# Sums of squares folded on VectorE, a third buffer for a tile of scales, and one integer step fewer in a streaming hybrid layer

## The chip, the cores and the metric

The kernel runs on one core of a Trainium2 chip. Its time is the device time of one execution in microseconds (us). The kernel before takes 2223.6 us, the median of three runs (2219.76, 2223.6 and 2225.92 us). The profiler took one more execution, which lasted 2219.34 us, and all lines of the profile come from that one.

TensorE (PE) multiplies matrices into PSUM. VectorE (DVE), ScalarE (ACT) and GpSimd (POOL) do the elementwise work. The queue of SyncE (SP) issues nearly all transfers.

## The reference, cut to what matters

One layer on 2112 tokens of width 1024 (2048 prompt frames and 64 frames of a running stream): a norm, one input projection, a gated delta rule and a pooling group, an output projection, a residual add, a second norm, a gated feed-forward part, a residual add and a final norm. The change touches how operands are brought into range for 16-bit products, above all in the feed-forward part, whose hidden width is 22 tiles of 128:

```python
h = rmsnorm(x, norm2_w)
x = x + (silu(h @ w_gate) * (h @ w_up)) @ w_down
```

## The kernel before, in words

**Precision.** A product in nearly full precision is made of three products of 16-bit parts. Every operand x is split into a high part hi = f16(c·x) and a low part lo = f16(c·x − hi) (`split16`, lines 907 to 910: the high part on ScalarE, the low part on VectorE), and hi·hi, hi·lo and lo·hi are summed in PSUM. The scale c is a power of two that depends on the size of the operand, and it is found on the chip.

**Finding a scale.** `scale_of` (lines 621 to 627) starts from a tile `squares` of 128 partitions and n columns, each column being a sum of squares that ScalarE wrote with its accumulator. It copies the n columns to bf16 on VectorE (`cols`, with the names `sqb` or `sqe` in the profile), then issues n products on TensorE, one per column, each against the same 128x128 matrix of one value; they add up in one column of PSUM, so that all partitions hold the total. `half_power` (lines 614 to 619) then makes a power of two of the total with integer steps on the bits: add 1e-30 (PSUM to SBUF), shift right by one and mask to the exponent, subtract from a constant. The square root of the total is so halved in its exponent and inverted.

`scale_of` is called for:
- the 22 tiles of gate and up weights, n = 4 (`prep_strassen`, line 809; PSUM tile `ws`, result `pscale`);
- the 22 tiles of down weights, n = 2 (`down_scale`, line 903; `wd`, `dscale`);
- the 8 tiles of output-projection weights, n = 2 (`convert`, line 850; `wcwout`);
- the 15 groups of hidden activations, n = 2G, that is 8 or 4 (`factors`, line 1986; `ec`, result in the tile `es`);
- three single sums, n = 1 (lines 634 and 881).

`half_power` is also called for the 21 scales of the input projection together and for one scale of the output projection (lines 870 and 890).

**Feed-forward stage.** It runs from about 940 us to the end. The tokens are cut into three blocks b = 0, 1, 2 of 704, each of two halves of 352 columns. In each block the 22 hidden tiles are made one after the other (`gate_up`: seven Strassen products of 12 matmuls each, tiles `px`, `py`, `pz`), and they form six groups of sizes 4, 4, 4, 4, 2, 4. When the last tile of a group is made, `factors` (lines 1981 to 2005) finds the group's scale into `es`, a tile of six columns, and splits seven combinations of the hidden tiles per pair into the f16 tiles `hq` and `h7` (seven operations on ScalarE and seven on VectorE for a pair; four subtractions on GpSimd before them). Later `down_strassen` (lines 2007 to 2027) multiplies the parts with the down weights (tiles `dx`, `dy`, `dz`) and adds the results into the residual tiles `y` with VectorE, and each of these additions reads a column of `es`. The down products of groups 0, 1 and 2 come one hidden tile after their group is complete; those of groups 3, 4 and 5 all come at the end of the block. Block 0 treats groups 0 and 4 without this scale, and block 2 group 5.

**Buffers.** `es` has two buffers, `h7` four, the f32 scratch tag `t` eight (`tmp` in `factors`, and the loads of the next block's hidden inputs, `xh`, share it). A third `es` tile can be written only when the first is released by its last reader.

**Order.** Nothing is issued as it is written. The class `Machine` records every operation, models engines and buffers, and writes out its own order for each engine (line 374, which is why all instructions have that line in the profile). It goes through the list in windows of 1000 operations and plays each window 40 times with randomly moved ranks from one generator with a fixed seed, and keeps the ranks that lose the least TensorE time (`issue`, lines 192 to 215; `play`, line 312). On each engine the instructions then run in that order. A product with one column counts as 3.4 ns of TensorE in this model (line 161).

Of the kernel before, what the change touches and what calls it, by code (L numbers as in the profile page):

```python
# [11 lines left out]
BF16 = mybir.dt.bfloat16  # L12
F32 = mybir.dt.float32
F32R = mybir.dt.float32r
AF = mybir.ActivationFunctionType
ALU = mybir.AluOpType
# [3 lines left out]
P = 128  # L20
# [44 lines left out]
class Machine:  # L65
# [126 lines left out]
    def issue(self):  # L192

        ops, self.ops = self.ops, []
        self.begin(ops)
        rand, stop = random.Random(1), 0
        while len(self.out) < len(ops):
            stop += WINDOW
            mine = [op for op in ops[max(0, stop - WINDOW - BEFORE) : stop + AFTER] if op.start is None and op.eng != "sync"]
            was, best = self.save(), None  # L200
            for i in range(PLAYS):
                ranks = [op.base for op in mine]
                if i:
                    hot = best[2] if i % 2 else ()
                    ranks = [r - rand.uniform(0, SPREAD) if op.order in hot and rand.random() < HOT else
                             r + rand.uniform(-SPREAD, SPREAD) if rand.random() < PART else r for op, r in zip(mine, best[1])]
                self.rank(mine, ranks)
                self.play(stop + AFTER)
                lost = self.free["tensor"] - self.work
                if best is None or lost < best[0]:  # L210
                    best = lost, ranks, self.culprits(was[2])
                self.restore(was)
            self.rank(mine, best[1])
            self.play(stop)
        self.emit(self.out)
# [93 lines left out]
                self.enter(op)  # L309
            self.serve(tag)  # L310

    def play(self, stop):

        wait, ready, total = self.wait, self.ready, self.total
        while len(self.out) < total and self.front < stop:
            best = None
            for e in self.free:
                if ready[e]:
                    t = self.free[e]
                    if e == "sync":  # L320

                        t = max(t, self.wire - (BACKLOG if ready[e][0][0] < self.front + AHEAD_OPS else IDLE))
                        if wait[e]:
                            t = min(t, max(self.free[e], wait[e][0][0]))
                elif wait[e]:
                    t = max(self.free[e], wait[e][0][0])
                else:
                    continue
                if best is None or t < best[0]:
                    best = (t, e)  # L330
            t, e = best
            while wait[e] and wait[e][0][0] <= t:
                op = heapq.heappop(wait[e])[2]
                heapq.heappush(ready[e], (op.rank, op.order, op))
            if e == "sync" and self.wire - (BACKLOG if ready[e][0][0] < self.front + AHEAD_OPS else IDLE) > t:
                continue
            if e == "tensor":
                op = self.pick(ready[e], t, wait[e])
                self.front = max(self.front, op.order)
                self.work += op.occ  # L340
            else:
                op = heapq.heappop(ready[e])[2]
            self.run(op, t)
            self.out.append(op)
            for nm in op.tiles:
                t = self.tiles[nm]
                t[2] -= 1
                t[3] = max(t[3], op.start + op.lat + 0.04)
                if not t[2]:
                    heapq.heappush(self.slots[t[0]], t[3])  # L350
                    self.serve(t[0])
                self.early -= t[4]
                self.gone = max(self.gone, t[3] if t[4] else 0.0)
            if not self.early and self.later:
                later, self.later = self.later, {}
                for tag, n in later.items():
                    self.slots[tag] = [self.gone] * n
                    self.serve(tag)
            for q in op.succs:
                self.touch(q)  # L360
                q.ready = max(q.ready, self.done(op, q))
                q.left -= 1
                if not q.left:
                    self.enter(q)
# [97 lines left out]
def hybrid_kernel(ctx, tc, a, o):  # L462
    nc = machine = Machine(tc.nc)
    act = nc.scalar.activation
    tt = nc.vector.tensor_tensor
    ts = nc.vector.tensor_scalar
# [4 lines left out]
    def cost(n, dt):  # L471
        clock["pe"] += n * (1.67e-3 if dt == F32 else 0.427e-3) + 0.005

    def mm(out, lhsT, rhs, start, stop, **kw):
        nc.tensor.matmul(out, lhsT, rhs, start=start, stop=stop, **kw)
        n = 1
        for d in out.shape[1:]:
            n *= d
        cost(n, rhs.dtype)
# [50 lines left out]
            c.step()  # L530

    ctx.enter_context(tc.manual_schedule())
    tc.nc.scalar.preload_act_table_set("natural_log_exp_and_others")

    def pool(name, where=ctx, early=False, behind=False, **kw):
        return Pool(machine, where.enter_context(tc.tile_pool(name=name, bufs=1, **kw)), early, behind)

    cpool, wpool, opool = pool("cpool"), pool("wpool"), pool("opool")
# [32 lines left out]
    for lo, n in S0:  # L571
        for i in range(2):
            nc.sync.dma_start(out=x0[i][:, :, lo : lo + n],
                              in_=a["xT"][4 * i : 4 * i + 4, :, lo : lo + n].rearrange("k p t -> p k t"))
# [20 lines left out]
    parts_b, five = {}, cpool.tile([P, 5], BF16, tag="onesb", name="onesb")  # L595
# [17 lines left out]

    def half_power(out, x):

        ts(out, x, TINY, None, ALU.add)
        bits = out.bitcast(mybir.dt.int32)
        ts(bits, bits, 1, 0x7F800000, ALU.logical_shift_right, ALU.bitwise_and)
        ts(bits, bits, -1.0, float(189 << 23), ALU.mult, ALU.add)

    def scale_of(out, squares, n, top, ps, tag="sqb"):

        cols = (cpool if tag == "sqb" else wq["pool"]).tile([P, 8], BF16, tag=tag, name=f"{tag}{machine.n}", bufs=2)[:, :n]
        nc.vector.tensor_copy(cols, squares[:, :n])
        for i in range(n):
            mm(ps[:, :1], parts_b[top], cols[:, i : i + 1], start=i == 0, stop=i == n - 1)
        half_power(out, ps[:, :1])

    def weigh_norms():
# [65 lines left out]
    for op in order:  # L695
        if op[0] == "gu":
            plan.append(("gu", op[2]))
            if op[1] == 1 and op[2] in PREP_AT:
                gi, m = PREP_AT[op[2]]
# [7 lines left out]
    wq = {}  # L707
# [1126 lines left out]
    f2 = pool("f2", behind=True)  # L1834
# [72 lines left out]
    def tmp(nm):  # L1907
        return f2.tile([P, N2], F32, tag="t", name=nm, bufs=TB)
# [72 lines left out]
    def factors(b, gi):  # L1981

        f0, G = groups[gi]
        es = einv[b, gi] = f2.tile([P, 6], F32, tag="es", name=f"es{b}_{gi}", bufs=2)
        c = es[:, :1]
        scale_of(c, esq.pop((b, gi))[:, : 2 * G], 2 * G, 2.0**13, psp.tile([P, 512], F32, tag="mm", name=f"ec{b}_{gi}", bufs=PSM), "sqe")
        nc.vector.reciprocal(es[:, 1:2], c)
        t = (f2.tile([P, 13, N2], F16, tag="hq2", name=f"hq{b}_{gi}", bufs=1) if G == 2 else
             opool.tile([P, 26, N2], F16, tag="op", name=f"hq{b}_{gi}", bufs=2))
        for p in range(G // 2):  # L1990
            f = f0 + 2 * p
            u, v = h3.pop(f), h3.pop(f + 1)
            low = f2.tile([P, N2], F16, tag="h7", name=f"h7{b}_{f}", bufs=4)
            part = {nm: (t[:, 13 * p + 2 * i], t[:, 13 * p + 2 * i + 1] if i < 6 else low) for i, nm in enumerate(FH)}
            gt = (nc.vector if f + 2 == NF else nc.gpsimd).tensor_tensor
            t3, t2, t4 = (tmp(f"q{i}{b}_{f}") for i in (3, 2, 4))
            for nm, x in (("11", u[:, 0]), ("21", v[:, 0]), ("22", v[:, 1])):
                split16(*part[nm], x, c)
            gt(out=t3, in0=v[:, 1], in1=u[:, 1], op=ALU.subtract)
            gt(out=u[:, 1], in0=u[:, 1], in1=u[:, 0], op=ALU.subtract)  # L2000
            gt(out=t2, in0=v[:, 1], in1=u[:, 1], op=ALU.subtract)
            gt(out=t4, in0=v[:, 0], in1=t2, op=ALU.subtract)
            for nm, x in (("T1", u[:, 1]), ("T2", t2), ("T3", t3), ("T4", t4)):
                split16(*part[nm], x, c)
            h3[f] = part
# [27 lines left out]
    h3, ys, esq, einv = {}, {}, {}, {}  # L2033
# [9 lines left out]
    for op in order:  # L2043
        b = op[1]
        if op[0] == "gu":
            f = op[2]
# [5 lines left out]
            gi = max(g for g, (f0, G) in enumerate(groups) if f0 <= f)  # L2052
            if b or gi >= min(STR0):
                if plain(b, gi):
                    if f == groups[gi][0] or f == groups[gi][0] + 2:
                        two = opool.tile([P, 2, 2, TB2], F32R, tag="op", name=f"h3l{f}", bufs=2)
# [61 lines left out]
PLAYS, WINDOW, BEFORE, AFTER, SPREAD, PART = 40, 1000, 200, 1000, 50, 0.02  # L2118
HOT, BACK = 0.5, 15.0
TABLE = 1.3  # L2120
TINY = 1e-30
# [122 lines left out]
```

## Time and profile before

| | |
|---|---|
| median of three runs | 2223.6 us |
| the profiled execution | 2219.34 us |
| its span, first to last instruction | 2217.6 us |
| granted TensorE clock, mean | 0.997 |
| TensorE busy | 2178.4 us (98%) |
| VectorE busy | 1597.9 us (72%) |
| ScalarE busy | 1364.6 us (62%) |
| GpSimd busy | 652.4 us (29%) |
| moved by DMA | 466 MB, 210 GB/s mean |

A line of a group names the engine, the operation, the tile written and the tiles read, the shape, the count, then busy time and mean duration, then the idle time of the engine just before and what ended it. A line of the timeline gives the start, the time covered, the engine, the operation and the count of equal instructions in a row; a bracket at its end is idle time before it and its releaser. A duration of a matmul holds its latency, so the distance between two starts tells the pace. A line of windows gives, for each stretch, the busy time of the engines with instruction counts, the granted clock of TensorE (PEclk), the DMA share and the rate.

### The profile page before, as it was taken

The page shows a single profiled execution, that of the slowest core. Times are in us where ns is not written, and L with a number is a line of the kernel's source. Part 1 is how long each engine was busy: PE and PEld are TensorE (multiplying, and loading weights), DVE is VectorE, ACT ScalarE, POOL GpSimd, SP SyncE. Part 2 cuts the span into 40 slices and gives each one's busy share as a digit, 9 for nine tenths or more (in the row PEclk, how much of TensorE's full clock was granted, in tenths as well). Part 3 has the DMA queues.
Part 4 walks back from the last instruction along what each step waited for, and adds up shares of the span by engine and source line. Part 5 has one row for each costly group of instructions (what it writes and reads, how often), then busy time and mean ns, then how long its engine had stood idle before and what let it go on. Part 6 is the DMA issues. An engine that isn't in the chain of part 4 may idle for free. (4 is left out here: it accounts for less than half of the span.)

```text
span 2217.6 us, 41377 instructions
## 1 busy us (share of the span) xinstructions
PE 2178.4 (98%) x14785; PEld 1535.4 (69%) x14785; DVE 1597.9 (72%) x3361; ACT 1364.6 (62%) x3235; POOL 652.4 (29%) x783
## 2 busy tenths in 40 slices
PE   8999999999999999999999999999999999999998
PEld 7999898767656666468666676666666566666667
DVE  7888785797779798688899977656543845445447
ACT  7998776787778996587666846732333343312414
POOL 3424342435335563021321117532101421100102
PEclk9999999999999999999999999999999999999999
DMA  7765577566664458996785668978545656444442
GB/s 280 245 213 172 163 269 268 174 211 230 212 216 145 143 157 285 303 333 238 232 295 205 216 204 288 341 244 265 156 143 158 201 186 220 154 145 151 140 140 72
DMA packets 222270, 466.41 MB, mean 210 GB/s; under 512 B 27504, under 2 KB 88944, under 8 KB 222064
## 3 DMA queue, kind: packets, MB, share of 16 engines
q1 hardware_dynamic: 221488, 463.06, 63.5%
q8 instruction: 115, 1.88, 0.3%
q14 instruction: 91, 0.75, 0.1%
q10 hardware_dynamic: 576, 0.72, 0.1%
HBM read 320.26 MB, written 143.43 MB: 209 GB/s over the span
## 5 line engine op out<-in xcount | busy, mean ns | idle before, releaser
L374 PE MATMUL pp<-h,wsp 128*128 128x288 f32 (+2 forms) x2480 | 517.9, 354 | 11.7 <-DVE wsp L374 10.2
L374 PEld LDWEIGHTS <-wsd 128*128 128x128 f16 x2352 | 229.7, 98 | 127.5 <-issue 6.2
L374 PEld LDWEIGHTS pp<-h,wsp 128*128 128x128 f32 x1488 | 226.8, 191 | 27.0 <-ACT wsp L374 8.7
L374 PE MATMUL dx<-hq,wsd 128*128 128x352 f16 x1232 | 233.0, 314 | 1.8 <-DVE y L374 1.5
L374 PEld LDWEIGHTS <-ws11S 128*128 128x128 f16 x1584 | 153.7, 98 | 83.0 <-ACT ws11S L374 1.5
L374 PEld LDWEIGHTS <-wsS 128*128 128x128 f16 x1584 | 154.1, 98 | 82.3 <-issue 2.0
L374 PEld LDWEIGHTS <-wsS3S 128*128 128x128 f16 x1584 | 154.3, 98 | 81.2 <-issue 0.5
L374 POOL TENSOR_TENSOR q<-hr,hr 128x352 f32<-128x352 f32 x52 | 53.9, 1036 | 444.6 <-DVE hr L374 391.2
L374 PEld LDWEIGHTS <-wsp 128*128 128x128 f16 x1184 | 109.1, 98 | 106.8 <-issue 2.7
L374 DVE SCALAR_TENSOR_TENSOR y<-dx,es,y 128x352 f32<-128x352 f32 x240 | 136.0, 580 | 63.7 <-PE dx L374 62.8
L374 ACT COPY g<-px 128x352 f32<-128x352 f32 x132 | 58.4, 443 | 190.3 <-PE px L374 188.9
L374 ACT ACTIVATE hr<-g,pscale 128x352 f32<-128x352 f32 x132 | 76.6, 586 | 143.3 <-DVE g L374 143.0
L374 PE MATMUL pz<-op,wsp 128*128 128x288 f32 (+2 forms) x768 | 158.6, 347 | 0.0
L374 PE MATMUL px<-hA,ws11S 128*128 128x352 f16 x792 | 139.2, 313 | 0.3 <-DVE ws11S L374 0.2
L374 PE MATMUL py<-hA,ws11S 128*128 128x352 f16 x792 | 137.9, 313 | 0.9 <-ACT ws11S L374 0.9
L374 PE MATMUL pz<-hA,wsS 128*128 128x352 f16 x792 | 136.5, 312 | 0.0
L374 PE MATMUL py<-hA,wsS3S 128*128 128x352 f16 x792 | 134.4, 312 | 0.3 <-ACT u L374 0.3
L374 PE MATMUL px<-hA,wsS 128*128 128x352 f16 x792 | 130.8, 312 | 1.4 <-ACT g L374 1.3
L374 PE MATMUL px<-hB,ws 128*128 128x352 f16 x792 | 130.2, 312 | 1.1 <-DVE u L374 0.9
L374 PE MATMUL px<-hA,wsS3S 128*128 128x352 f16 x792 | 130.6, 313 | 0.0
L374 PE MATMUL dy<-hq,wsd 128*128 128x352 f16 x672 | 124.9, 313 | 3.0 <-ACT hq L374 2.3
L374 ACT CAST TV_p<-pt_p 128x512 f16<-128x512 f32 x192 | 110.0, 586 | 23.3 <-PE pt_p L374 20.2
(797 smaller groups left out, 4838.6 us busy)
## 6 DMA issues: line engine op xcount, KB each, us to landing
ws11S<-g SPq DMA_DIRECT2D x44, 512.0 KB, 3.8
wsS<-g SPq DMA_DIRECT2D x44, 512.0 KB, 3.6
wsS3S<-g SPq DMA_DIRECT2D x44, 512.0 KB, 3.6
wrp<-in_win_dram SPq DMA_DIRECT2D x84, 256.0 KB, 3.5
wnd<-wsp SPq DMA_DIRECT2D x42, 512.0 KB, 4.9
wsp<-wnd SPq DMA_DIRECT2D x42, 512.0 KB, 4.0
wsd<-dn SPq DMA_DIRECT2D x40, 512.0 KB, 3.6
xd<-x2d SPq DMA_DIRECT2D x96, 176.0 KB, 3.9
```

Of the source, the lines that this page charges most:

```text
L374: getattr(getattr(self.nc, op.eng), name)(*args, **kw)
```

## The change

Three edits. `scale_of` sums the n columns with one reduction on VectorE, written as one bf16 column, and issues one product in place of n. `half_power` no longer adds 1e-30: the shift reads the bits of the total directly. `es` gets three buffers. Besides, a play of the order's search now ends once it has lost as much as the best one; a play's loss only grows, so no choice among given plays is changed by that. But as the recorded list gets shorter, the windows of the search and its random draws fall on other operations.

```diff
@@ issue / play: a play stops once it can't be the best
-                self.play(stop + AFTER)
+                self.play(stop + AFTER, best[0] if best else None)
...
-    def play(self, stop):
+    def play(self, stop, limit=None):
...
             self.out.append(op)
+            if limit is not None and self.free["tensor"] - self.work >= limit:
+                return
...
@@ hybrid_kernel
     ctx.enter_context(tc.manual_schedule())
+    ctx.enter_context(tc.nc.allow_low_precision(reason="sums of squares that choose a power of two"))
...
     def half_power(out, x):
 
-        ts(out, x, TINY, None, ALU.add)
         bits = out.bitcast(mybir.dt.int32)
-        ts(bits, bits, 1, 0x7F800000, ALU.logical_shift_right, ALU.bitwise_and)
+        ts(bits, x.bitcast(mybir.dt.int32), 1, 0x7F800000, ALU.logical_shift_right, ALU.bitwise_and)
         ts(bits, bits, -1.0, float(189 << 23), ALU.mult, ALU.add)
 
     def scale_of(out, squares, n, top, ps, tag="sqb"):
 
-        cols = (cpool if tag == "sqb" else wq["pool"]).tile([P, 8], BF16, tag=tag, name=f"{tag}{machine.n}", bufs=2)[:, :n]
-        nc.vector.tensor_copy(cols, squares[:, :n])
-        for i in range(n):
-            mm(ps[:, :1], parts_b[top], cols[:, i : i + 1], start=i == 0, stop=i == n - 1)
+        cols = (cpool if tag == "sqb" else wq["pool"]).tile([P, 8], BF16, tag=tag, name=f"{tag}{machine.n}", bufs=2)[:, :1]
+        nc.vector.tensor_reduce(out=cols, in_=squares[:, :n], op=ALU.add, axis=mybir.AxisListType.X)
+        mm(ps[:, :1], parts_b[top], cols, start=True, stop=True)
         half_power(out, ps[:, :1])
...
@@ factors
-        es = einv[b, gi] = f2.tile([P, 6], F32, tag="es", name=f"es{b}_{gi}", bufs=2)
+        es = einv[b, gi] = f2.tile([P, 6], F32, tag="es", name=f"es{b}_{gi}", bufs=3)
```

## The prediction

> **What bounds the kernel now.** I read the page first, then the list of who waited for whom, then the stretches by windows, and last the timeline around the places that the change touches. The page says which engine matters:
>
> ```profile
> span 2217.6 us, 41377 instructions
> PE 2178.4 (98%) x14785; PEld 1535.4 (69%) x14785; DVE 1597.9 (72%) x3361; ACT 1364.6 (62%) x3235; POOL 652.4 (29%) x783
> PE 30%; DVE 1%; DMA 0%; issue 0%; POOL 0%; ACT 0%; SPq 0%; DVEq 0%; POOLq 0%; ACTq 0%
> ```
>
> TensorE is busy for 2178.4 of 2217.6 us, and the chain that ended last runs through it alone (only 30% of the span is followed, but 1% is all that another engine has of it). So time comes from two places: TensorE work that goes away, and gaps in TensorE that close. VectorE, ScalarE and GpSimd count only where TensorE waits for them. The three windows below (busy time with instruction counts of PE, PEld, DVE, ACT, POOL, then the granted clock, the DMA share and GB/s) show where gaps are left. The first is where TensorE is slackest away from the kernel's ends, the second where VectorE is fullest, the third the end of block 1.
>
> ```profile
> 500.00:800.00 300.00, 291.78 (x1899) 187.15 (x1898) 241.96 (x520) 252.37 (x621) 141.50 (x189) 1.00 0.59 188
> 940.00:1240.00 300.00, 298.31 (x2059) 205.82 (x2057) 272.95 (x560) 222.97 (x490) 60.27 (x54) 1.00 0.75 259
> 1700.00:1800.00 100.00, 95.74 (x632) 61.83 (x630) 62.67 (x125) 32.58 (x75) 30.00 (x35) 0.97 0.59 188
> ```
>
> In 500 to 800 us TensorE has 300 − 291.78 = 8.2 us of gaps. In the third, 4.3 us are missing in 100, and the clock is below 1. That stretch holds the only long stall of the feed-forward stage, and it belongs to the change.
>
> **Part 1: one product per scale.** The groups of one-column products, and the VectorE operations around them:
>
> ```profile
> L374 PE MATMUL ws<-sqb,onesb x88: 163/163/178, 927.6 to 1268.1; 128*128 128x1 bf16 x88
> L374 PE MATMUL wd<-sqb,onesb x44: 163/164/178, 297.0 to 1483.7; 128*128 128x1 bf16 x44
> L374 PE MATMUL wcwout<-sqb,onesb x16: 163/163/167, 813.4 to 876.1; 128*128 128x1 bf16 x16
> L374 PE MATMUL ec<-sqe,onesb x112: 163/163/167, 1071.6 to 2094.3; 128*128 128x1 bf16 x112
> ```
>
> These are 88 + 44 + 16 + 112 = 260 products for 22 + 22 + 8 + 15 = 67 scales, so 260 − 67 = 193 go. Each row says 163 ns, but that is latency. The price is the distance between starts, read where eight of them stand in a row:
>
> ```profile
> 1071.56 0.34 PE L374 MATMUL ec<-sqe,onesb 128*128 128x1 bf16 x8
> 1071.76 1.35 PE L374 MATMUL py<-hA,wsS3S 128*128 128x352 f16 x8
> 1693.76 1.95 PE L374 MATMUL px<-hA,wsS 128*128 128x352 f16 x12
> 1695.55 1.95 PE L374 MATMUL pz<-hA,wsS 128*128 128x352 f16 x12
> ```
>
> Eight products take 1071.76 − 1071.56 = 0.20 us, 25 ns each; their weight loads are hidden behind the matmuls ahead of them. The other two lines give the pace of a normal matmul, for later: (1695.55 − 1693.76)/12 = 0.149 us. The removed work is 193 × 25 ns = 4.8 us, all of it on TensorE. It is worth its full length where TensorE has no gap around it, which holds for the feed-forward stage (298.31 of 300 us busy); 24 of the 193 lie before 900 us, for the 8 scales of `wcwout` and 16 of the 22 of `wd` (the row below counts their copies); they are 0.6 us, and I count them too. Bounds: nothing where the product filled a gap, 4.8 us as the whole. I take 4.8.
>
> ```profile
> L374 DVE CAST sqb<-sqp x16: 160/244/831, 295.3 to 795.8; 128x2 bf16<-128x2 f32 x16
> ```
>
> **Part 2: the reduction and the missing step on VectorE.** The copy becomes a reduction of the same columns, and one of three small steps goes:
>
> ```profile
> L374 DVE CAST sqe<-esq x15: 154/607/901, 1066.5 to 2089.6; 128x8 bf16<-128x8 f32 x13, 128x4 bf16<-128x4 f32 x2
> L374 DVE TENSOR_SCALAR es<-ec x15: 142/157/159, 1072.3 to 2094.5; 128x1 f32<-128x1 f32 x15
> ```
>
> No reduction is in this trace. The nearest row is the copy of the same columns: 154 ns at its shortest, 901 ns at its longest. So the reduction may gain 0.75 us a time or lose as much against today's copies; I take 0.16 us, the short end, as the columns are the same 8 elements. The step that goes is the add, 157 ns, once per scale. Both lie off the path: VectorE has 300 − 272.95 = 27 us free where it is fullest, and the weights have time. For gate and up weights the cover is seen here:
>
> ```profile
> 1142.30 1.28 DVE L374 SCALAR_TENSOR_TENSOR ws11S<-gr,pscale,ws11S 128x512 f16<-128x512 f32 x1
> 1149.82 1.51 PE L374 MATMUL px<-hA,ws11S 128*128 128x352 f16 x9
> ```
>
> The first low part is begun 7.5 us before the product that reads the new tile. A step shorter by 0.16 us, or a reduction longer by 0.75 us, vanishes in that, so I cost both at nothing; without the cover the two together would move a chain by at most 0.9 us. The shift now reads PSUM instead of SBUF; the add it replaces read the same PSUM column, so no new wait arises. The shorter plays of the search cost nothing on the chip, as they run before it.
>
> **Part 3: the third buffer of es.** In block 1 the groups 3, 4 and 5 all keep their `es` until the end of the block, and with two buffers the third has to wait. The timeline shows it in full:
>
> ```profile
> 1721.65 0.34 PE L374 MATMUL ec<-sqe,onesb 128*128 128x1 bf16 x8
> 1744.04 0.58 DVE L374 SCALAR_TENSOR_TENSOR y<-dy,es,y 128x352 f32<-128x352 f32 x1
> 1744.53 0.15 DVE L374 TENSOR_SCALAR es<-ec 128x1 f32<-128x1 f32 x1
> 1745.15 2.03 ACT L374 ACTIVATE hq<-hr,es 128x352 f16<-128x352 f32 x4 [3.48 <-DVE es L374]
> 1747.66 0.61 PE L374 MATMUL dy<-hq,wsd 128*128 128x352 f16 x3
> 1750.58 0.31 PE L374 MATMUL dy<-hq,wsd 128*128 128x352 f16 x1 [2.31 <-ACT hq L374]
> 1751.60 0.74 PE L374 MATMUL dy<-hq,wsd 128*128 128x352 f16 x2 [0.71 <-DVE hq L374]
> 1753.58 2.21 PE L374 MATMUL dx<-hq,wsd 128*128 128x352 f16 x7 [1.24 <-DVE y L374]
> 1755.59 0.50 PE L374 MATMUL dx<-h,wsd 128*128 128x352 f16 x1
> 1755.88 0.79 PE L374 MATMUL dx<-hq,wsd 128*128 128x352 f16 x2
> 1756.47 0.50 PE L374 MATMUL dx<-h,wsd 128*128 128x352 f16 x1
> 1756.76 1.43 PE L374 MATMUL dx<-hq,wsd 128*128 128x352 f16 x5
> 1758.03 0.61 PE L374 MATMUL dy<-hq,wsd 128*128 128x352 f16 x3
> 1750.00:1760.00 10.00, 7.47 (x33) 3.98 (x33) 8.95 (x19) 6.74 (x16) 7.58 (x9) 0.66 0.73 218
> 1722.00:1744.00 22.00, 22.00 (x149) 14.44 (x148) 15.49 (x28) 2.87 (x6) 5.22 (x7) 1.00 0.63 200
> ```
>
> The total of group 5 is in PSUM by about 1721.9, but the step that writes `es` starts at 1744.53, right behind the last additions into `y` of the group that held the buffer: 22 us late. The splits follow only then, and TensorE runs out of down products. From 1747.66 to 1758.03, 10.37 us, it starts 3 + 1 + 2 + 7 + 1 + 2 + 1 + 5 = 22 matmuls, which at 0.149 us are 3.28 us. The stall costs 10.37 − 3.28 = 7.1 us: 2.31 + 0.71 + 1.24 = 4.3 us of gaps, and the rest because the matmuls after them are slow (seven and the next start take 2.01 us, 0.287 us each) at a granted clock of 0.66.
>
> Those rows price the slow clock with the stall. [...]
>
> What is next late once `es` is free at 1722? ScalarE has 22 − 2.87 = 19 us free up to 1744 and needs 14 splits of about 0.5 us; VectorE has 22 − 15.49 = 6.5 us for 14 splits, and the shortfall of about half a microsecond is due only at 1748. Nothing is queued behind the wait any more. The scratch tiles that the splits hold come free about 20 us earlier, so the loads for block 2, which share them, are helped. One resource stays short: `h7` has four tiles and groups 3, 4 and 5 want five, so the low part of the last combination of group 5's second pair still waits for group 3's last product. That part is read only by the seventh product of a pass, six products of six matmuls (6 × 6 × 0.149 = 5.4 us) after the pass begins, so it does not bind. I take the whole 7.1 us; bounds 0 (another buffer holds it) and 7.1.
>
> **Sum.** 4.8 + 7.1 = 11.9 us. Against the profiled execution: 2219.34 − 11.9 = 2207.4 us (its span 2217.6 plus 1.7 us around it). That execution lies 4.3 us below the median of the runs, whose low end it matches, so I set the difference against the median: 2223.6 − 11.9 = 2211.7 us, or 0.54% less. About 0.3%, 6.7 us, is what a measurement of this kernel can tell from no change, so "faster" means below 2216.9 and "slower" above 2230.3.
>
> **The rivals.**
> 1. *The stall stays*, as another buffer (`h7`, the scratch tiles) binds in the place of `es`. For it: five `h7` tiles are wanted. Against it: the reader comes 5.4 us later. Then only the products count: 2223.6 − 4.8 = 2218.8 us, within 0.3%. Chance 0.11.
> 2. *The order is drawn anew.* The recorded list is shorter by some 260 operations, so every window of the search differs. In 500 to 800 us, where TensorE has the 8.2 us of gaps, a less lucky order might have half as much again and more; 5.5 us more would leave 2217.2 us, within 0.3%. Against it: the objective of the search is the same. Chance 0.07.
> 3. *The products were free.* Then only the stall comes back: 2223.6 − 7.1 = 2216.5 us, barely faster. Against it: the start after the eight comes 0.20 us late. Chance 0.04.
> 4. *Slower: the reduction is long and VectorE becomes the bound.* The place is 940 to 1240 us, where VectorE has 27 us free and 17 + 3 = 20 scales are found:
>
> ```profile
> L374 DVE TENSOR_SCALAR pscale<-ws x17: 140/150/159, 947.8 to 1230.1; 128x1 f32<-128x1 f32 x17
> L374 DVE TENSOR_SCALAR es<-ec x3: 149/150/158, 1072.3 to 1230.6; 128x1 f32<-128x1 f32 x3
> ```
>
>    Reductions of 0.16 + 27/20 = 1.5 us each would fill it; to undo the 11.9 us and add 6.7 takes 18.6/20 = 0.93 us more each. It decides from 2.4 us per reduction, giving 2230.3 us or more. Against it: the longest copy of the same columns takes 0.90 us. Chance 0.04. [...]
>
> **How the numbers follow.** The forecast has the remaining 0.74. It is faster, as is rival 3: 0.78. Rivals 1 and 2 are the same: 0.18. Rival 4 is slower: 0.04. The range reaches up to rival 1, 2219, and down to the lowest run of before less the sum and half of the gaps in 500 to 800: 2219.8 − 11.9 − 4.1 = 2203.8, so 2204. What it leaves out is rival 4 and a luckier or less lucky order than that.
>
> **What would show it.** Right: the groups `ws`, `wd`, `wcwout` and `ec` with 22, 22, 8 and 15 products; a reduction of about 0.16 us with no long ones; at the end of block 1 the step that writes `es` right behind the product `ec`, no gap of over 1 us before a `dy` or `dx`, and a clock of 1.00 throughout; TensorE busy for about 4.8 + 2.8 = 7.6 us less, and gaps lower by about 4.3 us. Wrong: reductions near 1 us and over; a wait for `h7` or a scratch tile in the old place; gaps in 500 to 800 us well over 8.2 us.

## The result, and the profile after

The changed kernel takes 2211.97 us (median of five runs, 2210.41 to 2214.72) against 2221.96 us for the kernel before on the same occasion. The ratio is 0.9955, 95% interval 0.994 to 0.997: 10.0 us or 0.45% faster. The forecast was 11.9 us less.

The page of the changed kernel, its span and the busy time of each engine (its profiled execution took 2213.56 us, a little over its median, while that of the kernel before lay at the low end of its runs; so the two spans differ by less than the medians):

```profile
span 2211.8 us, 40877 instructions
PE 2171.7 (98%) x14592; PEld 1531.6 (69%) x14592; DVE 1586.9 (72%) x3289; ACT 1364.1 (62%) x3235; POOL 652.8 (30%) x783
```

TensorE has 193 matmuls fewer (14785 to 14592) and is busy for 6.7 us less, where the forecast named 7.6. VectorE has 72 instructions fewer (3361 to 3289). The gaps on TensorE, span less busy time, didn't shrink by the 4.3 us that were forecast: they are 40.1 us, against 39.2 before. The groups of the scales, as rows by tile (count, then shortest, median and longest in ns):

```profile
L376 PE MATMUL ws<-sqb,onesb x22: 163/167/178, 933.7 to 1272.3; 128*128 128x1 bf16 x22
L376 PE MATMUL ec<-sqe,onesb x15: 167/167/167, 1077.3 to 2087.6; 128*128 128x1 bf16 x15
L376 DVE TENSOR_REDUCE sqe<-esq x15: 151/164/166, 1073.1 to 2083.0; 128x1 bf16<-128x8 f32 x13, 128x1 bf16<-128x4 f32 x2
L376 DVE TENSOR_REDUCE sqb<-sq x22: 142/149/160, 930.1 to 1269.0; 128x1 bf16<-128x4 f32 x22
```

There is one product per scale. In all its groups the reduction takes 0.13 to 0.17 us, where the copies went up to 0.9 us, so the long reduction that rival 4 needed didn't come.

The end of block 1, from the timelines of VectorE, ScalarE and TensorE, and the window in which the clock had dropped:

```profile
1722.38 0.16 DVE L376 TENSOR_SCALAR es<-ec 128x1 int32<-128x1 int32 x1
...
1724.07 2.06 DVE L376 SCALAR_TENSOR_TENSOR hq<-hr,es,hq 128x352 f16<-128x352 f32 x4
...
1729.52 1.07 DVE L376 SCALAR_TENSOR_TENSOR hq<-q,es,hq 128x352 f16<-128x352 f32 x2
1730.52 0.57 DVE L376 SCALAR_TENSOR_TENSOR y<-dx,es,y 128x352 f32<-128x352 f32 x1
```

```profile
1722.76 2.03 ACT L376 ACTIVATE hq<-hr,es 128x352 f16<-128x352 f32 x4 [2.02 <-DVE es L376]
```

```profile
1722.17 0.17 PE L376 MATMUL ec<-sqe,onesb 128*128 128x1 bf16 x1
...
1729.20 1.06 PE L376 MATMUL dy<-hq,wsd 128*128 128x352 f16 x6
1731.14 1.05 PE L376 MATMUL dz<-hq,wsd 128*128 128x352 f16 x6 [0.88 <-DVE y L376]
1732.04 0.61 PE L376 MATMUL dy<-hq,wsd 128*128 128x352 f16 x3
1732.82 2.40 PE L376 MATMUL dx<-hq,wsd 128*128 128x352 f16 x15 [0.17 <-DVE y L376]
```

```profile
1750.00:1760.00 10.00, 10.00 (x69) 6.56 (x67) 9.57 (x20) 3.68 (x8) 6.81 (x9) 1.00 0.74 241
```

The step that writes `es` now starts 0.2 us behind its product instead of 22.9 us, and the clock in 1750 to 1760 us is 1.00 instead of 0.66. But something is given back: from 1724.07 to 1730.52 VectorE does 13 splits in a row, ahead of the additions into `y`, and TensorE, whose next product waits for such an addition (the brackets of `dz` and `dx`), starts late twice. At 0.149 us a matmul the six at 1729.20 end their turn at 1730.09, so 1731.14 is 1.05 us late; the three at 1732.04 end theirs at 1732.49, so 1732.82 is 0.33 us late. That is 1.4 us of the 7.1.

Elsewhere the changed kernel is worse. The stretch before the feed-forward stage, windows of the kernel after and then of the kernel before:

```profile
700.00:930.00 230.00, 221.88 (x1417) 131.49 (x1417) 181.19 (x393) 173.69 (x429) 99.30 (x120) 0.99 0.63 206
```

```profile
700.00:930.00 230.00, 225.98 (x1469) 133.91 (x1469) 186.55 (x422) 178.55 (x440) 98.78 (x122) 1.00 0.68 214
```

TensorE has 8.1 us of gaps there instead of 4.0. The largest, and what follows it, in the timeline and the window of the kernel after:

```profile
714.84 0.80 PE L376 MATMUL pk_p<-vn_p,ktl_p 128*128 128x128 f32 x2 [3.42 <-ACT vn_p L376]
...
716.39 2.77 PE L376 MATMUL pp<-h,wsp 128*128 128x512 f16 x6
```

```profile
710.00:720.00 10.00, 6.58 (x30) 3.83 (x28) 4.67 (x8) 6.82 (x15) 6.91 (x8) 0.68 0.34 92
```

This is a wait of 3.42 us for a tile of the delta rule, which none of the edits touches, and behind it matmuls at half pace: the six at 716.39 cover 2.77 us, six of the same shape at 720.59 in the same timeline 1.46 us. The kernel before has no such wait there, and neither has the kernel below with all three edits in the old order. Progress is therefore read by stage. The table gives when a few products start, counted in each kernel's timeline (264 products `px<-hA,ws11S` make one block). Its last two columns belong to kernels of the experiments below.

| us from the span's start | before | after | all three edits, old order | reductions x8 |
|---|---|---|---|---|
| first gate product, block 0 | 929.9 | 938.0 | 926.0 | 955.0 |
| first gate product, block 1 | 1358.3 | 1360.1 | 1350.7 | 1397.3 |
| first gate product, block 2 | 1782.0 | 1778.2 | 1769.6 | 1814.9 |
| last gate product | 2140.4 | 2134.5 | 2125.6 | 2171.1 |
| span | 2217.6 | 2211.8 | 2203.0 | 2248.4 |

The changed kernel is 8.1 us behind at 938 us, wins 6.3 us in block 0, 5.6 in block 1 and 2.1 in block 2.

### The profile page after: what moved, and what is told of

Same layout as the page of the kernel before. It is cut to its first block, busy times and chain, and to the rows that moved or that the text cites. A ratio compares the mean times of both kernels' runs of the same rounds, so it can differ in the third digit from the quotient of the medians.

```text
span 2211.8 us, 40877 instructions
## 1 busy us (share of the span) xinstructions
PE 2171.7 (98%) x14592; PEld 1531.6 (69%) x14592; DVE 1586.9 (72%) x3289; ACT 1364.1 (62%) x3235; POOL 652.8 (30%) x783
## 4 chain that ended last, share of the span: by engine, by line
PE 53%; DVE 2%; ACT 1%; issue 0%; POOL 0%; DMA 0%; DVEq 0%; ACTq 0%; POOLq 0%
PE px L376 20%; PE py L376 10%; PE dx L376 9%; PE pz L376 5%; PE dy L376 4%; PE d L376 3%; PE dz L376 2%; DVE y L376 1%; DVE hq L376 1%; DMA wsd<-dn 0%; ACT junk L376 0%; DVE wsS3S L376 0%; PE rpnf L376 0%; POOL r L376 0%; DVE g L376 0%
## 5 line engine op out<-in xcount | busy, mean ns | idle before, releaser
L376 PE MATMUL dx<-hq,wsd 128*128 128x352 f16 x1232 | 228.4, 313 | 1.1 <-DMA wsd<-dn 0.9
```

What stands on the lines that cost most here:

```text
L376: getattr(getattr(self.nc, op.eng), name)(*args, **kw)
```

## The experiments

The difficulty is that any edit changes the order of the whole kernel. So several experiments keep the order of before: everything is recorded as before, the search runs on that, and only as the order is written down are operations exchanged or dropped. A kernel with a third buffer for `es` can keep the old order only up to about 1600 us; behind that its order is drawn anew. Theory: the products (4.8 us) and the stall (7.1 us) are the gain, and the new order takes some of it back. Rivals: the products were free, the stall's price has no slow clock in it, the gain is the luck of a draw, or small work on VectorE counts after all.

All ratios are to the kernel before on the same occasion, with 95% intervals. A ratio and the difference of two medians of a few runs can differ by a microsecond or so; where both are given, the interval belongs to the ratio.

| kernel | ratio | interval |
|---|---|---|
| changed kernel | 0.9955 | 0.994 to 0.997 |
| third buffer of es alone, old order up to 1600 us | 0.9978 | 0.9969 to 0.9986 |
| reduction and one product, old order | 0.9982 | 0.9974 to 0.9991 |
| reduction, still 260 products, old order | 0.9993 | 0.9984 to 1.0002 |
| the step left out, old order | 0.9984 | 0.9975 to 0.9994 |
| all three edits, old order up to 1600 us | 0.9931 | 0.9918 to 0.9945 |
| changed kernel, products x17 | 1.0066 | 1.0053 to 1.008 |
| changed kernel, reductions x8 | 1.0139 | 1.0123 to 1.0154 |
| before, second and third seed | 0.9984, 0.9981 | 0.9975 to 0.9993, 0.9973 to 0.999 |
| changed, second and third seed | 0.9902, 0.9949 | 0.9889 to 0.9916, 0.9936 to 0.9963 |

**The third buffer alone.**

```diff
-        es = ... f2.tile([P, 6], F32, tag="es", name=f"es{b}_{gi}", bufs=2)
+        es = ... f2.tile([P, 6], F32, tag="es", name=f"es{b}_{gi}", bufs=3)
```

> The kernel before with three buffers for es and nothing else; its order on each engine is that of before up to about 1600 us and new behind that. Theory (the stall at the end of block 1 costs 7.1 us with its slow clock): 7.1 us faster, ratio 0.9968, no gap over 1 us before a dy or dx near 1750 us and a granted clock of 1.00 there; the time to the first product of the feed-forward stage stays within 1 us of the 929.9 us of before. Rival, slow clock not part of the price: 4.3 us faster, ratio 0.9981. Rival, another buffer (h7, scratch) holds the splits: no change, a wait for it in the same place.

Median 2217.62 us against 2222.76 us: 5.1 us, interval 3.1 to 6.9 us. The stall is gone, and the same small waits as in the changed kernel have come in its place:

```profile
1734.05 1.05 PE L374 MATMUL dz<-hq,wsd 128*128 128x352 f16 x6 [0.81 <-DVE y L374]
```

7.1 less 1.4 us is 5.7, well inside the interval; the price without the slow clock, 4.3 less 1.4 or 2.9 us, is just outside. No other buffer took over. One sign was missed: the first gate product starts at 931.5 us, 1.6 us later than before and not within 1 us, behind a longer wait at about 800 us (2.19 us, where before it is 1.7) and a lower clock (0.91 in 790 to 810 us, before 1.00; the wait and the 0.91 are shown in the last section).

That the slow clock belongs to the stall is seen more directly in the windows of 1700 to 1800 us: the granted clock is 0.97 there in all six profiles of kernels with two buffers of `es`, and 1.00 in all seven with three. First the kernel before, then this one, then the stretch of the kernel before in which its clock was low:

```profile
1700.00:1800.00 100.00, 95.74 (x632) 61.83 (x630) 62.67 (x125) 32.58 (x75) 30.00 (x35) 0.97 0.59 188
1700.00:1800.00 100.00, 99.02 (x670) 64.84 (x669) 63.05 (x127) 34.60 (x78) 30.14 (x35) 1.00 0.61 194
1750.99:1757.82 6.83, 4.98 (x17) 2.48 (x17) 6.10 (x14) 4.96 (x13) 5.40 (x7) 0.50 0.68 210
```

**One product, in the old order.** The copy's place is taken by the reduction, product 0 reads its column, and the others are dropped:

```diff
         nc.vector.tensor_copy(cols, squares[:, :n])
+        machine.ops[-1].call = "tensor_reduce", (), dict(out=cols[:, :1], in_=squares[:, :n], op=ALU.add, ...)
         for i in range(n):
             mm(ps[:, :1], parts_b[top], cols[:, i : i + 1], start=i == 0, stop=i == n - 1)
+            machine.ops[-1].call = None if i else ("matmul", (ps[:, :1], parts_b[top], cols[:, :1]), dict(start=True, stop=True))
...
-        for op in out:
+        for op in (q for q in out if q.call):
```

> The kernel before in its own order on every engine, with the reduction in the place of each copy and with the 193 surplus products left out as the order is written down; es keeps two buffers, the add stays. Theory (a product costs 25 ns of TensorE on the path): 193 x 25 ns = 4.8 us faster, ratio 0.9978, the stall near 1750 us as before. Rival, the products filled gaps: no change, 0 us. Rival, what the changed kernel gained is all from its new order: no change either, but then the feed-forward stage, too, stays at the 1210.5 us that it takes before from its first to its last gate product.

Median 2218.05 us: 4.7 us faster (4.0 by the ratio), interval 2.0 to 5.8 us. That fits the forecast term, but the exchange of copy for reduction is in it too. The rival by which the products were free falls, unless the reduction alone brought the gain; that is tried below. TensorE's waits, from the list of who waited for whom (us in total, times, longest), first of this kernel, then of the one with all three edits:

```profile
PE dx L374 <- DVE y L374: 3.4, 4, 1.5
PE dy L374 <- ACT hq L374: 2.3, 1, 2.3
```

```profile
PE dx L374 <- DVE y L374: 0.9, 3, 0.4
```

The stall is still there (`dy` for `hq`), and in this one execution the waits of `dx` for additions into `y` are up to 3.4 us from 1.5 us before. Its stages therefore don't show the saving: from the first to the last gate product it takes 1209.7 us, against 1210.5 before. The gain rests on the times of the runs.

**All three edits, in the old order.** The edits of the two above, and in `half_power` the shift in the place of the add:

> All three edits of the change, but with the order of before kept up to about 1600 us (the surplus products and the add take part in the making of the order and are left out as it is written down). Theory (gains 4.8 + 7.1 us; the changed kernel's new order lost up to 8 us before 938 us): 11.9 us faster than before, ratio 0.9946, the first product of the feed-forward stage at about 929 us; faster than the changed kernel by up to 8 us. Rival, the time that the changed kernel shows before 938 us is scatter of single executions and not its order: no faster than the changed kernel, 0.9955.

Median 2205.99 us, 16.8 us faster than before; by the ratio it is 15.3 us, interval 12.2 to 18.2, just above the 11.9 of the forecast. The interval of the ratio (0.9918 to 0.9945) ends short of the changed kernel's 0.9955, whose own begins at 0.994. From 300 us to its first gate product the longest gap is 0.9 us. Two things follow. The order of the changed kernel costs it about 5 us (0.9955 against 0.9931, with some 4 us of uncertainty), and the table of stages shows where: this kernel starts the feed-forward stage at 926.0 us, the changed one at 938.0. And the edits are worth more than the forecast: third buffer and products together explain 9.8 us by medians, 8.9 by ratios.

**More products.** Each product of a scale is written 17 times in the changed kernel's order.

> The changed kernel in its own order, with each of the 67 products of a scale (and the three for single sums) issued 17 times in a row, each giving the same total again: 70 x 16 = 1120 products more. Theory (25 ns each on the path): 28 us slower than the changed kernel, near 2240 us, ratio to before near 1.008. Rival, products are free beside other work: no change, 2212 us. [...]

1.0066 against 0.9955 is 0.0111, or 24.7 us for 1120 products: 22 ns each (18 to 26 by the two intervals). So a product costs about its spacing on the path, the 25 ns that were read, and is not free. This kernel showed one more thing. It has the same wait in the delta rule as the changed kernel:

```profile
717.39 0.49 PE L378 MATMUL pk_p<-vn_p,ktl_p 128*128 128x128 f32 x2 [3.40 <-ACT vn_p L378]
...
718.22 1.46 PE L378 MATMUL pp<-h,wsp 128*128 128x512 f16 x6
```

```profile
710.00:720.00 10.00, 6.60 (x47) 4.03 (x46) 6.76 (x13) 6.95 (x15) 6.83 (x8) 1.00 0.43 141
```

The gap is 3.40 us, but the clock stays at 1.00 and the six matmuls behind it cover 1.46 us, not 2.77.

**The step alone.** The surplus of the kernel with all three edits had one candidate left, the term that the forecast had set to nothing.

```diff
         ts(out, x, TINY, None, ALU.add)
         bits = out.bitcast(mybir.dt.int32)
+        machine.ops[-1].call = "tensor_scalar", (bits, x.bitcast(mybir.dt.int32), 1, 0x7F800000, ALU.logical_shift_right, ALU.bitwise_and), {}
         ts(bits, bits, 1, 0x7F800000, ALU.logical_shift_right, ALU.bitwise_and)
+        machine.ops[-1].call = None
```

> The kernel before in its own order on every engine, with only the add of half_power left out (72 steps on VectorE fewer) as the order is written down; copies, 260 products and two buffers of es stay. Theory as predicted (the step is covered): no change, 0 us, ratio 1.000. Rival, formed on the kernel with all three edits in the order of before, which gained 16.8 us where es alone gave 5.1 and the products alone 4.7: the step is worth the missing 7 us, ratio 0.997, and shorter waits of TensorE for VectorE (pk_p for Sp, pp for wsp, dx for y).

Ratio 0.9984, interval 0.9975 to 0.9994: 3.6 us (1.3 to 5.6), not nothing, and about half of the 7 us that the rival named. The shorter waits that the rival asked for don't show: the profiled execution took 2221.05 us, over the median of 2217.69, with a longer wait for `Sp`. First this kernel, then the kernel before:

```profile
PE pk_p L374 <- DVE Sp L374: 4.2, 2, 3.8
PE pk_p L374 <- DVE Sp L374: 2.0, 2, 1.7
```

So that the step costs time is measured here; by which wait it does so is not. The parts now come to 0.0022 + 0.0018 + 0.0016 = 0.0056, the whole to 0.0069 (0.0055 to 0.0082): they don't contradict each other, each part being uncertain by some 0.0009.

**The reduction alone.** As in the kernel with one product, but all n products stay, each on the summed column.

> The kernel before in its own order, with the reduction in the place of each copy and still 260 products: each of the n products of a scale is issued on the one summed column and gives the same total again. Theory (the 4.7 us of the kernel with one product are the products): no change, ratio 1.000. Rival (VectorE's small work counts before 1360 us, and the copies, up to 0.9 us long, were part of it): 2 to 4 us faster, ratio 0.9985, and then the products are worth that much less than 4.8 us.

0.9993 with 1 inside the interval: the best value for the exchange of copy for reduction is 1.6 us, and it can't be told from nothing, nor from the lower half of the rival's 2 to 4 us. The products' own share, 0.9993 against 0.9982, is 2.4 us by this pair, with an uncertainty as large; the 22 ns of the other experiment give 193 x 22 ns = 4.2 us.

**Reductions eight times.** In the changed kernel's order, every reduction is written eight times.

> The changed kernel in its own order with every reduction issued 8 times in a row, each giving the same sum: 70 x 7 = 490 reductions more on VectorE, about 0.08 us apart, so some 0.6 us more per scale and 39 us of VectorE time in all. Theory as predicted (VectorE's work on a scale is covered): no change within 2 us, 2212 us. Rival, formed on the kernel with all three edits in the order of before (small steps on VectorE reach TensorE through the additions into y and the splits that stand behind them): 5 us slower or more.

1.0139: 41 us slower than the changed kernel, so the theory that this work is covered falls. One group in VectorE's timeline, then windows of this kernel:

```profile
1156.70 1.50 DVE L378 TENSOR_REDUCE sqb<-sq 128x1 bf16<-128x4 f32 x8
```

```profile
950.00:1300.00 350.00, 332.52 (x2196) 225.37 (x2196) 330.74 (x768) 251.24 (x549) 59.40 (x54) 1.00 0.70 243
1300.00:1800.00 500.00, 496.57 (x3324) 329.90 (x3322) 327.17 (x725) 227.48 (x514) 154.12 (x168) 1.00 0.69 227
```

and the matching window of the changed kernel:

```profile
938.00:1280.00 342.00, 341.70 (x2292) 234.16 (x2291) 319.27 (x628) 262.38 (x576) 63.55 (x58) 1.00 0.75 260
```

Eight reductions that write the same column take (1.50 − 0.16)/7 = 0.19 us each, so 490 of them are 94 us of VectorE, not the 39 that the expectation had. Of that, 41 us reach the end. The stages of the two profiled executions tell which, with the share of time for which VectorE is busy in the changed kernel (the first from 300 us on):

| stage | groups of eight | added on VectorE | lost | VectorE busy |
|---|---|---|---|---|
| up to block 0 | 29 | 39 us | 17.0 us | 77% |
| block 0 | 26 | 35 us | 20.2 us | 91% |
| block 1 | 10 | 14 us | −0.5 us | 58% |
| block 2 | 5 | 7 us | −0.1 us | 44% |

In the first two stages about half of the added work came through, in the last two none. The stages differ in more than VectorE's share (most weights are prepared in the first two), so the share is a hint and no threshold is shown.

In 950 to 1300 us TensorE has 17.5 us of gaps where the changed kernel has 0.3. Three of the longest waits in its list for the whole execution, which in the changed kernel are missing or under 0.3 us, are these:

```profile
PE px L378 <- ACT g L378: 6.1, 7, 2.0
PE px L378 <- DVE u L378: 4.3, 5, 1.4
PE wcwout L378 <- DVE sqb L378: 3.0, 3, 1.2
```

The third is a product that waits for its own reductions, and with `ws` and `wd` such waits for `sqb` come to 5.9 us. The first two are waits for other work. One of them can be followed through the queues:

```profile
1256.73 1.51 DVE L378 TENSOR_REDUCE sqb<-sq 128x1 bf16<-128x4 f32 x8
1258.75 0.58 DVE L378 SCALAR_TENSOR_TENSOR hr<-hr,pscale,u 128x352 f32<-128x352 f32 x1
1259.37 0.50 ACT L378 ACTIVATE junk<-hr 128x352 bf16<-128x352 f32 x1 [2.21 <-DVE hr L378]
1262.25 1.06 PE L378 MATMUL px<-hA,wsS 128*128 128x352 f16 x6 [1.99 <-ACT g L378]
```

The eight reductions stand ahead of `hr` on VectorE. ScalarE waits 2.21 us for `hr`, its copy of `g` stands behind that wait (it starts at 1261.77), and TensorE waits 1.99 us for `g`. None of the three belongs to the scale for which these eight reductions are done.

**Other seeds.** The search's generator starts from 2 and from 3, in the changed kernel and in the kernel before.

```diff
-        rand, stop = random.Random(1), 0
+        rand, stop = random.Random(2), 0
```

> The changed kernel with another seed for the search of its order, nothing else. Theory (the order drawn decides some us): another time than the 2212.0 us of the changed kernel by 3 to 8 us either way; before 930 us and not behind it if the place of the loss was the chunk stage. Rival, the order is worth nothing: 2212 us within 2 us.

> The kernel before with the other seed, nothing else. Theory (the order drawn decides some us): another time than 2222.8 us by 3 to 8 us either way, with the stall near 1750 us still there. Rival, the order is worth nothing: 2222.8 us within 2 us.

> The changed kernel with a third seed. Theory (an order is worth several us either way, and the first draw of the changed kernel was a poor one): between the 2199.8 us of the second seed and the 2212.0 us of the first. Rival (the first draw was an ordinary one): 2212 us or more.

> The kernel before with a third seed. Theory: between 2215 and 2226 us, the changed kernel faster than it by 10 us or more when both are taken over three seeds. Rival (part of the gain of the changed kernel is luck of the draws): under 2212 us.

The changed kernel with the second seed takes 2199.81 us, 20.9 us less than the kernel before and the fastest of all that ran. Its first gate product starts at 923.3 us, 14.7 us before that of the changed kernel, and its span is 13.9 us shorter: the difference lies before the feed-forward stage, as the theory had it. With the third seed the changed kernel takes 2212.34 us, as with the first. The two new draws of the kernel before are 0.16% and 0.19% faster than its first, and both still have the stall (TensorE waits 2.51 us at 1760.6 in the one, 3.56 us at 1751.1 in the other). So an order is worth up to 12 us, more than the 3 to 8 that were expected. The page of the fastest:

```profile
span 2197.9 us, 40932 instructions
PE 2168.3 (99%) x14592; PEld 1528.8 (70%) x14592; DVE 1579.2 (72%) x3289; ACT 1365.4 (62%) x3235; POOL 654.2 (30%) x783
```

It has 29.6 us of gaps on TensorE, against 40.1 us for the changed kernel with its own seed. The expectation that the first draw of the changed kernel was a poor one fell with the third seed: of the three draws, two lie together and the second stands out.

## Why the prediction was right, and where not

**What bounds the kernel** was right: time came and went on TensorE, as removed matmuls, as gaps and as clock.

**One product per scale, 4.8 us:** 4.7 us by medians (2.0 to 5.8), with the reduction in it, in the old order. The price of 25 ns holds; 1120 more products cost 22 ns each (18 to 26).

**The reduction's duration** was right: 0.16 us was taken, 0.13 to 0.17 measured.

**The step that goes, costed at nothing,** is the step that failed: "Both lie off the path: VectorE has 300 − 272.95 = 27 us free where it is fullest, and the weights have time." 72 steps were worth 3.6 us (1.3 to 5.6). Why is shown by the reductions eight times over, which cost 41 us for 94 added, all of it before block 1: the 7.5 us of cover were read for the weights that the scale itself serves, but the reductions also delayed other work that stood behind them on VectorE: in that kernel's trace `hr` starts 2.02 us after the first of the eight reductions ahead of it, ScalarE waits 2.21 us for `hr`, and TensorE 1.99 us for `g`. That the 72 steps acted by the same path is inferred, as their own profile doesn't show it. So free time counted over 300 us was not cover. Rival 4 was right that longer reductions could reach TensorE, and wrong on the point from which: it was to decide from 2.4 us per reduction, but 1.34 us more per scale cost 41 us. If the cost grows in proportion, an estimate, its 18.6 us would have come at about 0.16 + 1.34 x 18.6/41 = 0.8 us, within the length of some of the copies that went.

**The stall, 7.1 us:** it went as described, with the clock, but the term was too large: 5.1 us were measured (3.1 to 6.9). The part on what is next late was half wrong: the shortfall of VectorE was seen, but put at 1748 us, where the data are due; it came at 1731 us, as the order puts the 13 splits ahead of the additions. 1.4 us came back as that wait. Because the order behind 1600 us was drawn anew, a part of the 5.1 us may be the draw. No product waited for `h7`, as argued.

**The slow clock in the price of the stall** was worth 2.8 us of the 7.1. The time of the third buffer alone, faster by 3.1 to 6.9 us, speaks for it, if narrowly; the profiles do so plainly, with the low clock at the stall in all six kernels that have it (0.97 in the mean of 1700 to 1800 us) and in none of the seven that don't (1.00). Elsewhere, at 710 to 720 us, the changed kernel did run at a low clock (0.68).

**The order drawn anew** had a chance of 0.07 as a rival that would leave the time the same. It did happen, beside the forecast and not in its place: about 5 us were lost. The sign named for it, gaps in 500 to 800 us well over 8.2 us, did not show: they are 7.1 us. The long wait at 714 us lies in that stretch, with its slow clock, but other gaps there closed, and the loss shows in 700 to 930 us. That the search keeps its objective was no argument; the draws of one kernel differ by up to 0.5%.

So that the total of 11.9 us came near the measured 10.0 was in part luck. A step worth 3.6 us was left out, the stall was put 2 us too high, and an order that cost about 5 us took back what the edits brought beyond the forecast, and more. Over three draws of each kernel the mean ratios are 0.9988 and 0.9935, a difference of 0.0053 or 11.8 us; with draws that scatter by 0.3% this is uncertain by some 4 us either way (one standard error, an estimate).

## What to carry to other kernels

Free time of an engine in a window is not cover: here eight reductions on VectorE, 1.51 us, passed on through other work behind them to a wait of TensorE of 1.99 us. So price small steps on a well-filled engine at some share of their length, and test the share by writing them several times. Here it was about half where VectorE was 77% and 91% busy, and nothing where it was 58% and 44% busy. Where a search or a scheduler redraws the order at every edit, compare edits in a kept order and over several draws before a few tenths of a per cent are called a gain. A buffer that is released late took more here than its gaps, 7.1 us by the trace for 4.3 us of gaps, as the matmuls behind it ran at a low clock (0.50 in 1750.99 to 1757.82 us). And the work that moves up when it is released can stand ahead of other work: here 13 splits ahead of the additions for which TensorE waited (0.88 and 0.17 us).

## What the runs showed of the hardware

The same gap of TensorE (3.42 us in the changed kernel, 3.40 us with its products written 17 times, at the same place in the same order) came with a clock of 0.68 in the window of 10 us in one execution and of 1.00 in the other; six matmuls behind it covered 2.77 us in the one and 1.46 us in the other. The two are different kernels with one profiled execution each, so what made the difference is not shown by them. Shorter gaps came with a low clock too: at the stall at 1750 us the longest gap was 2.31 us and the clock in the window of 10 us was 0.66, and in the kernel with the third buffer alone the clock was 0.91 in the mean of 20 us around a gap of 2.19 us, the longest there:

```profile
799.16 0.49 PE L374 MATMUL pk_p<-Sp,Yqk 128*128 128x128 f32 x2 [2.19 <-DVE Sp L374]
```

```profile
790.00:810.00 20.00, 17.82 (x119) 11.00 (x118) 14.83 (x35) 16.40 (x38) 11.20 (x16) 0.91 0.50 137
```

So a gap of 3.4 us came once with a slow stretch and once without one, and gaps of 2.19 and 2.31 us came with one. What decides it is not shown here.
